# A two-layer decoder trunk on one core: compressed scores, their transposes and the nonlinearity's transposes at other places of a hand-written order, the last squares on DVE, the second weight block as two loads

## The chip, the core and the metric

The kernel runs on one core of a Trainium2 chip. The core has a matrix engine (TensorE, PE, with a separate weight load, PEld), a vector engine (VectorE, DVE), a scalar engine (ScalarE, ACT), a general engine (GpSimd, POOL) and a queue engine (SyncE, SP) that here only issues DMAs. Each engine takes its own instructions in order; engines wait for one another through semaphores. The metric is the device time of one execution in microseconds, as the median over runs.

## What is computed

The input x is 256 tokens by 1024. Layer 0 is stick-breaking attention and a squared-ReLU MLP. After it, shared keys and values are projected for three branches. Layer 1 is native sparse attention (NSA) over these and a second MLP. A last RMSNorm ends the trunk. All data are fp32. The parts that the change touches, cut from the reference:

```
hid   = gelu(einsum('bncgf,cfe->bncge', blk, cmp_w1))       # compressed blocks, hidden layer
cmp   = einsum('bncge,ced->bncgd', hid, cmp_w2)             # k_cmp, v_cmp: 15 blocks of 4 groups
sc    = einsum('bqghd,bngd->bghqn', qg, k_cmp) * scale      # compressed scores
p_cmp = softmax(where(valid_c, sc, NEG))
o_cmp = einsum('bghqn,bngd->bqghd', p_cmp, v_cmp)
...
out   = einsum('bsch,bschd->bshd', gates, [o_cmp, o_sel, o_win])   # sigmoid gates, then @ w_o
h     = h + out @ w_o
h     = h + relu(rms_norm(h, g) @ w1)**2 @ w2
return rms_norm(h, final_norm)                               # h * rsqrt(mean(h*h) + eps) * gain
```

With 256 tokens the selected and the window branch each run over all causal keys, so the kernel computes plain causal softmax scores for both.

## The kernel before

Weights are streamed from HBM by SP in blocks of up to 1 MB (`raw`). Each fp32 block is split into two fp32r tensors: ACT makes the high part (L125, CAST `wh<-raw`), DVE the rest (L126, `wl<-raw,wh`). PE multiplies such products in three passes (L177, L178, L179: high by high, and the two cross products; which of the two operands is the low one differs by the caller). Other products are single fp32 passes (L182), and transposes are matmuls with the identity (L185).

**The start.** `v_load` loads a part of a block of the value weights wv. The block of index 0 holds the rows for k = 0 and k = 1, 1024 columns each; k = 0 is loaded in two halves of 512 columns, k = 1 in one piece. `x_load` loads x by k, ACT and DVE scale and split it (L412, L413), and `pv` is accumulated over k by three matmuls for each of two token tiles and two column halves, twelve for each k. All these loads are issued by SP in the order of the code.

**Layer 1.** The table `NSA` is an order of steps written out by hand, and PE's instructions keep exactly that order (`keep_in_program_order`). The orders of DVE, ACT and POOL come from the scheduler, which places each step's instructions by its own costs. The steps that matter here:

- `('q', g, half)`: half of the query projection of group g, 24 matmuls into `pq`; after the second half ACT copies it to `qu` (L721). `('qr', g)`: rotary tables applied to it (L726 to L730 on DVE, L727 on POOL), giving `qr`.
- `('ge',)`: the nonlinearity of the hidden layer, which ends in `hu` on DVE (L758). `('ch',)`, `cmp_hid`: four PE transposes of hu into `pht` (L765), the copy `hidT` on ACT (L767), and its widened copy `hv` on POOL (L769). `('ck',)`, `cmp_kv`: PE products `pkc` from hidT and `pvc` from hv, then DVE copies to `kcb` (L781) and `vcb` (L788).
- `('cp', hf)`, `cmp_probs`: the compressed scores `psc` of half of the heads on PE, and their softmax: DVE L805, L807, ACT L809 (exponential), DVE L811 to L815, into `ce`. `('ct', hf)`, `cmp_tr`: four PE transposes of ce into `pct` and the ACT copy `pcT` (L824); the second argument names the PSUM pool of pct ("a" or the default "z").
- For each pair p of heads: `('S', p)` scores `z` on PE, each with a mask and minimum on DVE (L857) and an exponential with its sum on ACT (L859); `('M', p)` one over the sums times the gate on DVE (L866, L868, tile `rs`), then four multiplies of the tiles `pe` by rs on POOL (L873); `('T', p)` twelve transposes `ptp` and their copies `pT` (L888 on DVE, L890 on ACT); `('V', p)` the products with the values, into `po`, the last of them with pcT and vcb.
- `('w',)`: one more split of a weight block, `('o', ...)`: the output projection.

**The tail.** The second MLP ends in `finish`, called for each token tile t, each half n of the 1024 columns and each piece q of that half. For the last tile the second half comes as 384 and 128 columns. Each call takes the squares with their sum on ACT (L972) and multiplies by the gain on DVE (L973). After the second half the sum becomes `v` (L978), POOL raises it to the power -0.5 (L983), ACT scales columns 0 to 383 and DVE the other 640 (L985, L986), and ACT and SP issue one output DMA each (L987, L988).

Of the kernel before, what the change touches and what calls it, by code (L numbers as in the profile page):

```python
# [7 lines left out]
F32 = mybir.dt.float32  # L8
F32R = mybir.dt.float32r
BF16 = mybir.dt.bfloat16  # L10
AF = mybir.ActivationFunctionType
OP = mybir.AluOpType
AX = mybir.AxisListType

P = 128
D = 1024
T = 2
# [37 lines left out]
def hybrid_kernel(ctx, tc, x, xcols, eye, gcols, gfin, wqk, wv, wo0, wkv, wq, wg, rot, wo1, w1, w2, cw1, cw2, cpos, gate_b, consts, out):  # L55
    nc = tc.nc

    cp = ctx.enter_context(tc.tile_pool(name="cp", bufs=1))
    wp = ctx.enter_context(tc.tile_pool(name="wp", bufs=3))
    sp = ctx.enter_context(tc.tile_pool(name="sp", bufs=2))  # L60
# [7 lines left out]
    def big(shape, dt, name):  # L68
        return cp.tile(shape, dt, tag="e", name=name, bufs=3)
# [35 lines left out]
    def v_load(j, a, b):  # L105
        nc.sync.dma_start(raws[j][:, a:b], stream[j][0][:, a:b])
# [100 lines left out]
    hres = [cp.tile([P, D], F32, name=f"hres{t}") for t in range(T)]  # L207
# [6 lines left out]
    npow = cst[:, C_PW:C_PW + 1]  # L214
# [165 lines left out]
    def layer0(ap):  # L380
# [5 lines left out]
        v = big([P, T, D], F32, "v0")  # L386
# [15 lines left out]
        def x_load(k, m):  # L402
            nc.sync.dma_start(xin[:, k:k + m, :].rearrange("p k q -> p (k q)"), xcols[:, k * T * P:(k + m) * T * P])
# [17 lines left out]
        v_load(0, 0, 512)  # L421
        v_load(0, 512, D)
        x_load(1, 1)
        v_load(0, D, 2 * D)
        x_load(2, 1)
        v_load(1, 0, D)
        x_load(3, 1)
# [520 lines left out]
    def scoped(f, name, *a, bufs=2):  # L948
        with tc.tile_pool(name=name, bufs=bufs) as ap:
            return f(*a, ap)  # L950

    xn = scoped(layer0, "l0")
    nxt = []

# [8 lines left out]
    gf = big([P, D], F32, "gf")  # L963
# [4 lines left out]
    def finish(i, t, n, q):  # L968
        c = slice(n * 512 + q.start, n * 512 + q.stop)
        j = n + (q.start > 0)  # L970
        ss, sq, y = ssq[t], ys[t][:, 0, :], ys[t][:, 1, :]
        nc.scalar.activation(sq[:, c], hres[t][:, c], AF.Square, accum_out=ss[:, j:j + 1])  # L972
        nc.vector.tensor_mul(y[:, c], hres[t][:, c], gf[:, c])  # L973
        if n == 0:
            nc.vector.tensor_scalar(ss[:, 0:1], ss[:, 0:1], 1.0 / D, EPS, op0=OP.mult, op1=OP.add)
            return
        v = sp.tile([P, 1], F32, name="v", bufs=4)
        nc.vector.scalar_tensor_tensor(v, ss[:, j:j + 1], 1.0 / D, ss[:, 0:1], op0=OP.mult, op1=OP.add)  # L978
        if q.stop < 512:
            nc.vector.tensor_copy(ss[:, 0:1], v)  # L980
            return
        r = sp.tile([P, 1], F32, name="r", bufs=4)
        nc.gpsimd.tensor_tensor(r, v, npow, op=OP.pow)  # L983
        m = 384
        nc.scalar.activation(y[:, 0:m], y[:, 0:m], AF.Copy, scale=r)  # L985
        nc.vector.tensor_scalar(y[:, m:D], y[:, m:D], r, None, op0=OP.mult)  # L986
        nc.scalar.dma_start(out[t * P:(t + 1) * P, 0:m], y[:, 0:m])  # L987
        nc.sync.dma_start(out[t * P:(t + 1) * P, m:D], y[:, m:D])  # L988

    scoped(mlp, "m1", 1, 3, xn, finish)  # L990


# [92 lines left out]
```

## Time and profile before

| | us |
|---|---|
| median of 3 runs | 626.78 (626.08 to 626.88) |
| profiled execution | 626.89 |
| its span on the core | 625.1 |
| PE busy in the span | 613.3 (98%) |
| DVE busy | 416.7 (67%) |
| ACT busy | 344.6 (55%) |
| POOL busy | 54.1 (9%) |
| mean granted PE clock | 0.998 |

A row of a timeline gives the start, the busy time, the engine, the line, the operation, the output and inputs by the program's names, the shapes and the count, and in brackets the idle time before it and what ended it. A row of a view of waits gives who waited for whom, then the total, the times and the longest in microseconds. Line numbers are those of the kernel before; in the changed kernel most stand one higher.

### The profile page before, as it was taken

How to read it: one execution, taken by the hardware profiler on the slowest of the kernel's cores; microseconds unless marked ns; L12 is line 12 of the kernel's file. 1: busy time of each engine (PE TensorE's matmuls, PEld its weight loads, DVE VectorE, ACT ScalarE, POOL GpSimd, SP SyncE). 2: the span in 40 equal slices, each digit the busy share in tenths (PEclk: the TensorE clock that was granted, in tenths of full speed). 3: DMA queues.
4: the chain of work that ended last, by engine and by line, in shares of the span. 5: the costliest groups of instructions: out<-in, count | busy, mean ns of one | idle time of the engine just before them, and what ended most of it. 6: DMA issues, size and time to landing. Idle time of an engine off the chain costs nothing.

```text
span 625.1 us, 9055 instructions
## 1 busy us (share of the span) xinstructions
PE 613.3 (98%) x3555; PEld 516.1 (83%) x3555; DVE 416.7 (67%) x667; ACT 344.6 (55%) x593; POOL 54.1 (9%) x76
## 2 busy tenths in 40 slices
PE   8999999999999999999999998999999999999995
PEld 5899987888888888888888786777888888888885
DVE  5588887766566666656774798854676656666655
ACT  5666666464554444443853686773564455444442
POOL 0100000000000000000321166450000000000000
PEclk9999999999999999999999999999999999999999
DMA  8863333546555455553558511212374555545501
GB/s 299 342 264 136 135 135 135 170 163 207 201 185 204 159 202 193 202 202 135 175 210 329 202 69 69 102 40 96 135 231 174 201 202 190 204 156 201 194 0 68
DMA packets 17755, 108.12 MB, mean 173 GB/s; under 512 B 2352, under 2 KB 3504, under 8 KB 5680
## 3 DMA queue, kind: packets, MB, share of 16 engines
q1 hardware_dynamic: 16416, 105.97, 47.5%
q10 hardware_dynamic: 1296, 1.57, 0.7%
q8 instruction: 28, 0.46, 0.3%
q14 instruction: 15, 0.12, 0.1%
HBM read 106.48 MB, written 1.05 MB: 172 GB/s over the span
## 4 chain that ended last, share of the span: by engine, by line
PE 90%; DVE 4%; ACT 2%; issue 1%; DMA 1%; SPq 0%; POOLq 0%; POOL 0%; DVEq 0%
PE pu L182 29%; PE acc L177 12%; PE acc L178 11%; PE acc L179 11%; PE po L182 3%; PE qk L177 3%; PE qk L179 2%; PE qk L178 2%; PE z L182 2%; PE pk L177 2%; PE pk L178 2%; PE pk L179 2%; PE ptp L185 1%; ACT pe L859 1%; PE ph L182 1%
## 5 line engine op out<-in xcount | busy, mean ns | idle before, releaser
L126 DVE TENSOR_TENSOR wl<-raw,wh 128x1024 fp32r<-128x1024 f32 (+1 forms) x190 | 225.9, 1224 | 124.1 <-ACT wh L125 116.3
L125 ACT CAST wh<-raw 128x1024 fp32r<-128x1024 f32 (+1 forms) x190 | 189.7, 1043 | 104.4 <-PE acc L179 51.1
L182 PE MATMUL pu<-xn,wh 128*128 128x512 f32 x512 | 132.1, 392 | 0.0
L182 PEld LDWEIGHTS pu<-xn,wh 128*128 128x128 f32 x512 | 93.7, 188 | 18.0
L177 PE MATMUL acc<-wh,hh 128*128 128x512 f32 (+1 forms) x256 | 100.2, 391 | 0.0
L178 PE MATMUL acc<-wl,hh 128*128 128x512 f32 (+1 forms) x256 | 99.9, 390 | 0.0
L179 PE MATMUL acc<-wh,hl 128*128 128x512 f32 (+1 forms) x256 | 99.0, 389 | 0.0
L182 PE MATMUL pu<-xn,wl 128*128 128x256 f32 x512 | 76.5, 282 | 0.0
L182 PEld LDWEIGHTS pu<-xn,wl 128*128 128x128 f32 x512 | 72.1, 190 | 5.1
L179 PEld LDWEIGHTS acc<-wh,hl 128*128 128x128 f32 x256 | 48.1, 188 | 10.7 <-DVE hl L355 0.6
L177 PEld LDWEIGHTS acc<-wh,hh 128*128 128x128 f32 x256 | 48.2, 188 | 10.1 <-ACT hh L354 0.9
L178 PEld LDWEIGHTS acc<-wl,hh 128*128 128x128 f32 x256 | 48.2, 188 | 8.7
L354 ACT CAST hh<-ms 128x512 fp32r<-128x512 f32 x32 | 19.8, 620 | 63.0 <-DVE ms L350 63.0
L346 ACT COPY mr<-pu 128x256 f32<-128x256 f32 x64 | 23.6, 368 | 27.7 <-PE pu L182 27.7
L177 PE MATMUL qk<-xa,wh 128*128 128x256 f32 x128 | 37.4, 292 | 0.0
L179 PE MATMUL qk<-xa,wl 128*128 128x256 f32 x128 | 36.3, 284 | 0.0
L178 PE MATMUL qk<-xa,wh 128*128 128x256 f32 x128 | 36.2, 283 | 0.0
L355 DVE TENSOR_TENSOR hl<-ms,hh 128x512 fp32r<-128x512 f32 x32 | 22.1, 691 | 19.2 <-ACT hh L354 19.2
L873 POOL TENSOR_TENSOR pe<-pe,rs 128x512 f32<-128x512 f32 (+1 forms) x32 | 31.4, 1013 | 21.8 <-DVE rs L868 16.4
L859 ACT ACTIVATE pe<-pe,nm 128x256 f32<-128x256 f32 (+1 forms) x64 | 28.3, 443 | 8.4 <-DVE nm L857 7.2
L347 DVE TENSOR_TENSOR mu<-pu,mr 128x256 f32<-128x256 f32 x64 | 26.6, 417 | 7.5 <-ACT mr L346 7.5
L177 PE MATMUL acc<-wh,oT 128*128 128x512 f32 x64 | 26.2, 409 | 0.0
(187 smaller groups left out, 851.0 us busy)
## 6 DMA issues: line engine op xcount, KB each, us to landing
raw<-in_w SPq DMA_DIRECT2D x64, 1024.0 KB, 4.8
raw<-in_wqk SPq DMA_DIRECT2D x8, 1024.0 KB, 4.9
raw<-in_wo SPq DMA_DIRECT2D x8, 1024.0 KB, 4.7
raw<-in_wkv SPq DMA_DIRECT2D x6, 1024.0 KB, 4.9
raw<-in_wq SPq DMA_DIRECT2D x4, 1024.0 KB, 4.9
wc<-in_cw SPq DMA_DIRECT2D x4, 1024.0 KB, 6.7
raw<-in_wv SPq DMA_DIRECT2D x7, 512.0 KB, 8.8
hres<-in_x SPq DMA_DIRECT2D x2, 512.0 KB, 8.9
```

What stands on the lines that cost most here:

```text
L125: nc.scalar.copy(h[:, r], raws[j][:, r])
L126: nc.vector.tensor_sub(lo[:, r], raws[j][:, r], f32(h[:, r]))
L177: pe(nc.tensor.matmul(o, a[0], b[0], start=first, stop=False, skip_group_check=True))
L178: pe(nc.tensor.matmul(o, a[0], b[1], start=False, stop=False, skip_group_check=True))
L179: pe(nc.tensor.matmul(o, a[1], b[0], start=False, stop=last, skip_group_check=True))
L182: pe(nc.tensor.matmul(o, a, b, start=first, stop=last, skip_group_check=True))
L346: nc.scalar.copy(r[:, q], pu[:, 256:512])
L347: nc.vector.tensor_add(u[:, q], pu[:, 0:256], r[:, q])
L354: nc.scalar.copy(hh, sv)
L355: nc.vector.tensor_sub(hl, sv, f32(hh))
L859: nc.scalar.activation(e, e, AF.Exp, scale=-1.0, bias=nm[:, hd, t, b:b + 1], accum_out=rs[:, hd, t, b:b + 1])
L873: nc.gpsimd.tensor_tensor(sv, sv, rs[:, hd, t, :][:, :, None].to_broadcast([P, 2, n]), op=OP.mult)
```

## The change

Three edits. In the table of layer 1, `('ch',)` goes from ahead of `('q', 2, 0)` to behind it, `('cp', 0)` from behind T 1, qr 2 and a weight split to ahead of `('q', 3, 0)`, and `('ct', 0)` from behind `('q', 3, 1)` to ahead of it, with its PSUM tile from the other pool. At the start the load of the second k is issued as two loads of 512 columns. In `finish`, for the second half of the columns one reducing DVE multiply replaces ACT's square, the gain multiply and the tile v; it starts from the sum so far and writes the next one. POOL takes that sum directly. The last scaling is divided at 512 columns instead of 384, and DVE's part now multiplies h by r and the gain in one instruction.

```diff
-    ('cw', 1, 0), ('cw', 1, 1), ('q', 1, 0), ('ge',), ('q', 1, 1), ('S', 0, 'zzaz'), ('M', 0), ('qr', 1), ('ch',),
-    ('q', 2, 0), ('S', 1), ('M', 1), ('ck',), ('q', 2, 1), ('w',), ('T', 0, 'zaa'), ('S', 2, 'azaz'), ('q', 3, 0),
-    ('T', 1), ('qr', 2), ('w',), ('cp', 0), ('M', 2), ('S', 3, 'azaa'), ('q', 3, 1), ('ct', 0, 'a'), ('M', 3), ('V', 0), ('S', 4),
+    ('cw', 1, 0), ('cw', 1, 1), ('q', 1, 0), ('ge',), ('q', 1, 1), ('S', 0, 'zzaz'), ('M', 0), ('qr', 1),
+    ('q', 2, 0), ('ch',), ('S', 1), ('M', 1), ('ck',), ('q', 2, 1), ('w',), ('T', 0, 'zaa'), ('S', 2, 'azaz'), ('cp', 0),
+    ('q', 3, 0), ('T', 1), ('qr', 2), ('w',), ('M', 2), ('S', 3, 'azaa'), ('ct', 0), ('q', 3, 1), ('M', 3), ('V', 0), ('S', 4),
...
-        v_load(0, D, 2 * D)
+        v_load(0, D, D + 512)
+        v_load(0, D + 512, 2 * D)
...
-        nc.scalar.activation(sq[:, c], hres[t][:, c], AF.Square, accum_out=ss[:, j:j + 1])
-        nc.vector.tensor_mul(y[:, c], hres[t][:, c], gf[:, c])
+        hv = hres[t]
         if n == 0:
+            nc.scalar.activation(sq[:, c], hv[:, c], AF.Square, accum_out=ss[:, 0:1])
+            nc.vector.tensor_mul(y[:, c], hv[:, c], gf[:, c])
             nc.vector.tensor_scalar(ss[:, 0:1], ss[:, 0:1], 1.0 / D, EPS, op0=OP.mult, op1=OP.add)
             return
-        v = sp.tile([P, 1], F32, name="v", bufs=4)
-        nc.vector.scalar_tensor_tensor(v, ss[:, j:j + 1], 1.0 / D, ss[:, 0:1], op0=OP.mult, op1=OP.add)
+        nc.vector.tensor_tensor_reduce(sq[:, c], hv[:, c], hv[:, c], 1.0 / D, ss[:, j - 1:j], OP.mult, OP.add, ss[:, j:j + 1])
         if q.stop < 512:
-            nc.vector.tensor_copy(ss[:, 0:1], v)
             return
         r = sp.tile([P, 1], F32, name="r", bufs=4)
-        nc.gpsimd.tensor_tensor(r, v, npow, op=OP.pow)
-        m = 384
+        nc.gpsimd.tensor_tensor(r, ss[:, j:j + 1], npow, op=OP.pow)
+        m = 512
         nc.scalar.activation(y[:, 0:m], y[:, 0:m], AF.Copy, scale=r)
-        nc.vector.tensor_scalar(y[:, m:D], y[:, m:D], r, None, op0=OP.mult)
+        nc.vector.scalar_tensor_tensor(y[:, m:D], hv[:, m:D], r, gf[:, m:D], op0=OP.mult, op1=OP.mult)
```

What the table makes of the engines' queues is seen at three places. First POOL, between the rotary product of group 1 (L727, in the changed kernel L728) and the multiplies of M1 (the last row). The tiles pe_3233 and pe_3234 before, pe_3234 and pe_3235 after, are those of M0. Before:

```order
L727 TENSOR_TENSOR qr_2659<-qu_2658,cs_2646 128x512 x2
L769 COPY hv_3269<-hidT_3267 128x480
L873 TENSOR_TENSOR pe_3233<-pe_3233,rs_3232 128x512
L873 TENSOR_TENSOR pe_3234<-pe_3234,rs_3232 128x512
L873 TENSOR_TENSOR pe_3233<-pe_3233,rs_3232 128x256
L873 TENSOR_TENSOR pe_3234<-pe_3234,rs_3232 128x256
L873 TENSOR_TENSOR pe_3310<-pe_3310,rs_3309 128x512
```

Of the change:

```order
L728 TENSOR_TENSOR qr_2660<-qu_2659,cs_2647 128x512 x2
L874 TENSOR_TENSOR pe_3234<-pe_3234,rs_3233 128x512
L874 TENSOR_TENSOR pe_3235<-pe_3235,rs_3233 128x512
L874 TENSOR_TENSOR pe_3234<-pe_3234,rs_3233 128x256
L874 TENSOR_TENSOR pe_3235<-pe_3235,rs_3233 128x256
L770 COPY hv_3299<-hidT_3297 128x480
L874 TENSOR_TENSOR pe_3311<-pe_3311,rs_3310 128x512
```

The copy hv moved from ahead of the four multiplies of M0 to behind them. Second PE, from the last matmul of q(2,0) to the first of q(2,1) in the changed kernel:

```order
L179 MATMUL pq<-xq,wl 128x256
L766 MATMUL pht<-ident,hu 128x60 x4
L182 MATMUL z_3301<-kT,qr 128x512
L182 MATMUL z_3302<-kT,qr 128x512
L182 MATMUL z_3303<-kT,qr 128x256
L182 MATMUL z_3304<-kT,qr 128x256
L182 MATMUL pkc<-hidT,w2d 128x60 x2
L182 MATMUL pvc<-cw2s,hv 60x64 x8
L177 MATMUL pq<-xq,wh 128x256
```

Before, the transposes pht stood ahead of q(2,0), so that its 24 matmuls came between pht and these four scores of S1; now only the four scores stand between pht and the products with hidT and hv. Third DVE, at the softmax of the first compressed scores. Before:

```order
L805 TENSOR_REDUCE cmx<-psc 128x16
L868 TENSOR_TENSOR rs<-rs,gates 128x8
L807 TENSOR_TENSOR ce<-psc,cmx 128x240
L857 ISA pe,nm<-z_3513,nmask 128x256
L857 ISA nm 128x1
L857 ISA pe,nm<-z_3513,nmask 128x256
L857 ISA nm 128x1
L811 TENSOR_REDUCE csm<-ce 128x16
```

Of the change, as far as the multiply that ends it:

```order
L806 TENSOR_REDUCE cmx<-psc 128x16
L727 STREAM_SHUFFLE qx<-qu 128x512
L808 TENSOR_TENSOR ce<-psc,cmx 128x240
L730 TENSOR_TENSOR qx<-qx,cs 128x512
L126 TENSOR_TENSOR wl<-raw,wh 128x1024
L812 TENSOR_REDUCE csm<-ce 128x16
L889 COPY pT<-ptp 128x512
L813 RECIPROCAL csm<-csm 128x16
L731 TENSOR_TENSOR qr<-qr,qx 128x512
L814 TENSOR_TENSOR csm<-csm,gates 128x16
L867 RECIPROCAL rs<-rs 128x8
L816 TENSOR_TENSOR ce<-ce,csm 128x240
```

Before, the steps of the softmax stood among the masked scores (L857) of S3; now the rotary steps of group 2, a weight split and a copy of pT stand between them, and S3's follow it.

## The prediction

> **What bounds the kernel now.** I read the page first, then TensorE's (PE's) waits where layer 1's order is edited, then the timelines of the engines it waits for, then the two ends.
>
> ```profile
> span 625.1 us, 9055 instructions
> PE 613.3 (98%) x3555; PEld 516.1 (83%) x3555; DVE 416.7 (67%) x667; ACT 344.6 (55%) x593; POOL 54.1 (9%) x76
> PE 90%; DVE 4%; ACT 2%; issue 1%; DMA 1%; SPq 0%; POOLq 0%; POOL 0%; DVEq 0%
> ```
>
> PE is busy 98% of the span and carries 90% of the chain that ended last. The change leaves its work as it is, so a change of time can only come from PE's few gaps, from new gaps, and from the two ends. In the edited stretch of layer 1 (356 to 392 us) the waits of PE and the busy times (PE, weight load, DVE, ACT, POOL; clock 1.00) are:
>
> ```profile
> PE pht L765 <- DVE hu L758: 1.3, 1, 1.3
> PE po L182 <- ACT pcT L824: 1.3, 1, 1.3
> PE pct L185 <- DVE ce L815: 0.3, 1, 0.3
> 356.00:392.00 36.00, 33.13 (x263) 26.04 (x261) 32.61 (x122) 29.13 (x96) 21.34 (x20) 1.00 0.23 86
> ```
>
> DVE, at 32.6 of 36 us, is almost as full as PE, and POOL, 9% over the span, is 59% busy here. An average over the whole kernel hides that. PE's timeline of the stretch:
>
> ```profile
> 358.96 0.46 PE L765 MATMUL pht<-ident,hu 60*128 60x60 f32 x4 [1.29 <-DVE hu L758]
> 359.35 0.38 PE L177 MATMUL pq<-xq,wh 128*128 128x256 f32 x1
> ...
> 362.41 1.56 PE L182 MATMUL z<-kT,qr 64*128 64x512 f32 x8
> 363.90 0.66 PE L182 MATMUL pkc<-hidT,w2d 128*128 128x60 f32 x4
> 364.49 1.10 PE L182 MATMUL pvc<-cw2s,hv 128*60 128x64 f32 x16
> ...
> 374.36 1.47 PE L185 MATMUL ptp<-ident,pe 128*128 128x128 f32 x12
> ...
> 377.38 0.28 PE L182 MATMUL psc<-cmb,cbf 128*128 128x120 bf16 x2
> 377.58 2.18 PE L182 MATMUL z<-kT,qr 64*128 64x512 f32 x8
> ...
> 383.14 0.60 PE L185 MATMUL pct<-ident,ce 128*60 128x128 f32 x4 [0.31 <-DVE ce L815]
> ...
> 386.45 0.65 PE L182 MATMUL po<-pcT,vcb 128*64 128x256 f32 x4 [1.26 <-ACT pcT L824]
> ```
>
> PE loses four pieces: 1.29 ahead of the transposes of the hidden layer (pht), 2.18 - 1.56 = 0.62 inside the scores of pair 3, 0.31 ahead of pct, and 1.26 ahead of the products with pcT. Together 3.48 us.
>
> **The change part by part.** *Layer 1's order.* The half projection q(2,0) lasts 362.41 - 359.35 = 3.06 us and now stands ahead of the transposes. It covers the 1.29 us in which hu is late. What is late next is what the transposes start: hidT on ACT, then hv on POOL, which pkc and pvc need. Before, q(2,0) and S1 (3.06 + 1.5 us of PE) stood between; now S1 alone does.
>
> ```profile
> 362.22 0.34 ACT L767 COPY hidT<-pht 128x240 f32<-128x240 f32 x1
> 362.46 1.05 ACT L125 CAST wh<-raw 128x1024 fp32r<-128x1024 f32 x1
> ```
> ```profile
> 361.00 1.20 DVE L126 TENSOR_TENSOR wl<-raw,wh 128x1024 fp32r<-128x1024 f32 x1
> ...
> 363.03 0.57 DVE L868 TENSOR_TENSOR rs<-rs,gates 128x8 f32<-128x8 f32 x1
> ...
> 363.92 1.34 DVE L730 TENSOR_TENSOR qr<-qr,qx 128x512 f32<-128x512 f32 x1
> ...
> 369.29 2.34 DVE L126 TENSOR_TENSOR wl<-raw,wh 128x1024 fp32r<-128x1024 f32 x2
> ```
> ```profile
> 362.62 0.94 POOL L769 COPY hv<-hidT 128x480 f32<-128x480 f32 x1 [2.44 <-ACT hidT L767]
> 363.68 3.63 POOL L873 TENSOR_TENSOR pe<-pe,rs 128x512 f32<-128x512 f32 x4
> 369.51 5.17 POOL L873 TENSOR_TENSOR pe<-pe,rs 128x512 f32<-128x512 f32 x4 [2.20 <-DVE rs L868]
> ```
> ```profile
> 379.55 3.18 POOL L873 TENSOR_TENSOR pe<-pe,rs 128x512 f32<-128x512 f32 x4 [3.62 <-DVE rs L868]
> ```
>
> On ACT the cast wh now stands ahead of hidT, so hidT is ready near 362.3 + 1.05 + 0.34 = 363.6 instead of 362.56. That alone would cost PE little, as pkc started at 363.90. POOL is the place that counts. Its rows above show that hv, which stood ahead of the four multiplies of M0, now stands behind them, and POOL takes its instructions in order. M0 needs rs (L868, begun at 363.03; its row lasts to 363.60, with hv running beside it). M0 then starts between 363.1 and 363.68, and I take 363.3. Its four multiplies last 3.18 us where DVE leaves them alone, 3.63 beside one L730, and 5.17 beside two L126 of 2.34 us. DVE now does one L126 and a L729 and L730 in that time. So I add 5.17 - 3.18 = 1.99 for two L126, that is 1.0 for one, and 0.2 for part of the 0.45 of L730. hv, 0.94, ends at 363.3 + 3.18 + 1.2 + 0.94 = 368.6. The lower bound is 363.1 + 3.18 + 0.94 = 367.2, the upper 363.68 + 5.17 + 0.94 = 369.8. pvc began at 364.49 before; it is **4.1 us** later (2.7 to 5.3). All of PE queues behind it: q(2,1), the transposes T0, S2.
>
> [...]
>
> While PE stands, DVE, ACT and POOL go on. The three later gaps, 0.62 + 0.31 + 1.26 = 2.19 us, are then recovered, and two edits help there: the scores psc move ahead of q(3,0), T1 and S3, and q(3,1), about 3 us, now covers the copy of pcT. Against that, the softmax chain of ce now shares DVE with L726, L729, an L126, L888 and L730 between its steps. It took 383.14 - 377.66 = 5.5 us from the end of psc to pct before. What covers it now is q(3,0), T1 and S3, 3.06 + 1.3 (T1's transposes, the row at 374.36) + 1.56 = 5.9 us, and one L126 is already 1.2 us more chain. I take 0.6 us of new waits there and at the later transposes (0 to 1.2: at the low end they fall into slack, at the high end the L126 lies in the chain whole). Pool z for pct instead of pool a costs no instruction.
>
> Layer 1's stretch: 4.1 - 2.19 + 0.6 = **+2.5 us** (0.5 to 4.3).
>
> *Second weight block in two.*
>
> ```profile
> 2.58 0.43 SPq L106 DMA_DIRECT2D raw<-in_wv  x1
> ```
> ```profile
> 4.32 0.62 ACT L125 CAST wh<-raw 128x512 fp32r<-128x512 f32 x1 [2.30 <-DMA raw<-in_wv]
> ...
> 8.82 1.14 ACT L125 CAST wh<-raw 128x512 fp32r<-128x512 f32 x2 [0.77 <-DMA raw<-in_wv]
> ```
> ```profile
> 9.49 1.02 PE L177 MATMUL pv<-wh,xa 128*128 128x512 f32 x3 [1.23 <-ACT wh L125]
> 10.36 0.40 PE L178 MATMUL pv<-wl,xa 128*128 128x512 f32 x1
> ...
> 12.44 0.84 PE L177 MATMUL pv<-wh,xa 128*128 128x512 f32 x3
> ```
>
> ACT idled 0.77 us for the block, so its cast could start at 8.05 at the earliest. With the first half landed midway the cast ends near 8.8, and the rest wl 0.7 later, about 9.5. PE's first matmul moves up, but the second needs wl: 9.53 plus 11 matmuls at (12.44 - 10.36) / 9 = 0.23 us ends at 12.05 instead of 12.44. That is **-0.4 us** (-0.5 to 0, the latter if the first half lands no earlier). The extra issue of 0.43 us on SP delays the second half and the loads queued behind it, x_load(2,1) first; the second half has six matmuls, 1.4 us, of cover, and without that the 0.43 would eat the gain.
>
> *Tail.*
>
> ```profile
> 618.35 0.28 PE L179 MATMUL accq<-wh,hl 128*128 128x128 f32 x1
> ```
> ```profile
> 619.00 0.15 DVE L980 COPY ssq<-v 128x1 f32<-128x1 f32 x1
> 619.07 0.34 DVE L268 SCALAR_TENSOR_TENSOR hres<-accq,r,hres 128x128 f32<-128x128 f32 x1
> 619.44 0.29 DVE L973 TENSOR_TENSOR ys<-hres,gf 128x128 f32<-128x128 f32 x1
> ```
> ```profile
> 620.12 0.55 POOL L983 TENSOR_TENSOR r<-v,cst 128x1 f32<-128x1 f32 x1 [5.22 <-DVE v L978]
> ```
> ```profile
> 620.70 0.62 ACT L985 ACTIVATE ys<-ys,r 128x384 f32<-128x384 f32 x1 [0.85 <-POOL r L983]
> 621.34 0.36 ACTq L987 DMA_DIRECT2D out<-ys  x1
> ```
>
> PE ends at 618.63, but the last residual (L268) starts at 619.07 behind v and L980, both gone. I put it at 618.7. One reducing multiply of 128 columns replaces ACT's square, its read, and v: priced by L973's 0.29 for the same shape, plus a read of 0.1, so POOL's power starts near 619.45 instead of 620.12. The last scaling grows from 384 to 512 columns, at most 0.62 x 512/384 = 0.83. Net -0.67 + 0.15: **-0.5 us** (-0.65 to -0.2).
>
> Sum against the profiled execution, 625.1 in the span and 626.89 in all: +2.5 - 0.4 - 0.5 = +1.6, so 628.5. It stands 0.1 above the median of the runs, 626.78, hence **628.4**.
>
> **The rivals.** *No change:* POOL is free of DVE, hv comes at its lower bound, and no new wait shows. Then layer 1 costs 2.7 - 2.19 = 0.5, less 0.9 at the ends: 626.4. With half a microsecond of contention or of waits left, about 627.2. For it: the four multiplies do run in 3.18 us where DVE is elsewhere. Against: DVE is 91% busy here, with two L126 due near. *Faster:* POOL does not hold pvc at all, because hv gets through before M0; then all of the 3.48 us go and the ends add 0.9: 622.5. It decides as soon as hv ends by 364.5, as before. For it speaks that hidT is ready at 363.6, with POOL idle at that moment if rs is late. Against it: an engine's queue does not overtake. *A cascade:* M0 and hv block L729 and L730 on DVE in turn (1.34 us in the row above), which delays S1's exponentials, M1 and ce; pvc at its upper bound and 1.2 us of waits give 5.3 - 2.19 + 1.2 = +4.3, less 0.9 or less: 630.2 to 630.9. For it: DVE has 3.4 us free in 36. Against: PE stands for 4 us meanwhile and gives DVE time to catch up.
>
> **How the numbers follow.** Forecast (a long stall at pvc, the later gaps recovered) 0.45, no change 0.30, cascade 0.17, faster 0.08. A measurement of this kernel tells a difference of about 0.2%, or 1.25 us, so "same" is 625.5 to 628.0. Slower holds the cascade and most of the forecast, 0.17 + 0.38 = 0.55; same holds the rest of the forecast and the no-change case, 0.37; faster 0.08. The forecast alone runs from 627.5 to 629.5; to hold eight in ten I go down to the no-change case, 626.6, and up to just under the cascade, 630.2.
>
> **What would show it.** Right: PE's wait ahead of pht is gone, and a wait of about 4 us stands at pvc, released by POOL's hv near 368.6; the 1.26 us at po<-pcT is gone; the first long wait of the start is 0.6 us shorter; the last DMA is issued about 2.2 us after PE's last matmul instead of 2.7. Wrong: pvc starts by 366, or hv stands ahead of M0 on POOL in the trace (then faster), or new waits over 1.2 us at pct, S3 or the ptp transposes (then the cascade). If the start or the tail moves by more than half a microsecond the other way, those terms were mis-sized.

## The result, and the profile after

| | before | changed |
|---|---|---|
| median of 6 runs each, us | 626.83 (626.08 to 627.0) | 631.13 (629.87 to 632.04) |
| ratio | 1 | 1.007 (95% interval 1.0057 to 1.0083) |
| profiled execution, us | 626.89 | 629.87 |
| span, us | 625.1 | 628.0 |
| mean granted clock of PE | 0.998 | 0.991 |

The change made the kernel 4.3 us slower. The forecast of 628.4 had the direction, and the range ended at 630.2, below the result. First PE's waits of the changed kernel in the stretch of layer 1 (350 to 400 us):

```profile
PE pvc L182 <- POOL hv L770: 4.4, 1, 4.4
PE pkc L182 <- ACT hidT L768: 1.1, 1, 1.1
PE ptp L185 <- DVE nm L858: 0.7, 1, 0.7
```

The waits at pht, at pct and at the products with pcT are gone, and the wait at pvc is there. In PE's timeline:

```profile
355.16 1.56 PE L182 MATMUL z<-kT,qr 64*128 64x512 f32 x8
...
362.60 0.66 PE L182 MATMUL pkc<-hidT,w2d 128*128 128x60 f32 x4 [1.08 <-ACT hidT L768]
367.63 1.96 PE L182 MATMUL pvc<-cw2s,hv 128*60 128x64 f32 x16 [4.38 <-POOL hv L770]
...
369.52 0.58 PE L177 MATMUL pq<-xq,wh 128*128 128x256 f32 x1
...
373.33 1.47 PE L185 MATMUL ptp<-ident,pe 128*128 128x128 f32 x12
```

Layer 1's first scores start at 355.16 instead of 356.11, so all of this stretch is to be read 0.95 us earlier. The rows of before for this are:

```profile
356.11 1.56 PE L182 MATMUL z<-kT,qr 64*128 64x512 f32 x8
...
368.49 1.47 PE L185 MATMUL ptp<-ident,pe 128*128 128x128 f32 x12
```

Against the first scores pvc starts 12.47 us later instead of 8.38 (364.49 - 356.11): 4.1 us later, just as worked out. But the same matmuls of pvc (eight, which the trace shows as sixteen records) now last 1.96 us instead of 1.10, and from pvc to the transposes ptp it is 5.70 us where it was 4.00 (364.49 to 368.49). The same work on PE takes 1.70 us longer, with no wait in it. The windows tell why (the columns are those of the prediction's window: busy times of PE, PEld, DVE, ACT, POOL, then the granted clock, the share of DMA and GB/s):

```profile
362.00:367.00 5.00, 0.66 (x4) 0.52 (x4) 4.91 (x19) 2.17 (x9) 4.63 (x5) 0.76 0.52 162
367.00:368.00 1.00, 0.37 (x4) 0.37 (x5) 0.56 (x5) 1.00 (x5) 0.57 (x2) 0.50 0.57 238
...
370.00:371.00 1.00, 1.00 (x7) 1.00 (x7) 1.00 (x5) 0.00 (x0) 0.00 (x0) 0.50 0.00 0
371.00:372.00 1.00, 1.00 (x8) 1.00 (x8) 0.18 (x2) 0.00 (x0) 0.68 (x1) 0.79 0.00 0
372.00:373.00 1.00, 1.00 (x11) 1.00 (x10) 0.00 (x0) 0.00 (x0) 1.00 (x2) 1.00 0.04 8
```

While PE stood, its granted clock fell to 0.50, and it came back only at about 371.4, after 3.8 us of work at 0.50. POOL's queue is what held hv:

```profile
362.37 4.66 POOL L874 TENSOR_TENSOR pe<-pe,rs 128x512 f32<-128x512 f32 x4 [3.14 <-ACT wh L125]
366.98 0.59 POOL L770 COPY hv<-hidT 128x480 f32<-128x480 f32 x1
```

M0 takes 4.66 us (I had 3.18 + 1.2) and hv 0.59 (I had 0.94). The start and the tail:

```profile
11.46 0.84 PE L177 MATMUL pv<-wh,xa 128*128 128x512 f32 x3
...
621.58 0.28 PE L179 MATMUL accq<-wh,hl 128*128 128x128 f32 x1
```
```profile
624.09 0.38 ACTq L987 DMA_DIRECT2D out<-ys  x1
```

k = 2 starts at 11.46 instead of 12.44 in this execution. The last output DMA is issued 624.09 - 621.86 = 2.23 us after PE's last matmul, instead of 621.34 - 618.63 = 2.71.

### The profile page after: what moved, and what is told of

Same layout as the page of the kernel before. It is cut to its first block, busy times and chain, and to the rows that moved or that the text cites. A ratio compares the mean times of both kernels' runs of the same rounds, so it can differ in the third digit from the quotient of the medians.

```text
span 628.0 us, 9044 instructions
## 1 busy us (share of the span) xinstructions
PE 614.5 (98%) x3555; PEld 518.2 (83%) x3555; DVE 414.4 (66%) x666; ACT 343.3 (55%) x587; POOL 53.9 (9%) x76
## 4 chain that ended last, share of the span: by engine, by line
PE 93%; ACT 2%; DVE 2%; issue 1%; POOL 1%; POOLq 0%; DVEq 0%; ACTq 0%
PE pu L182 28%; PE acc L177 11%; PE acc L178 11%; PE acc L179 11%; PE po L182 3%; PE qk L177 3%; PE qk L179 2%; PE qk L178 2%; PE z L182 2%; PE pk L177 2%; PE pk L178 2%; PE pk L179 2%; PE ptp L185 2%; PE pv L177 1%; PE pv L178 1%; PE pv L179 1%
```

## The experiments

The theory after the result: the stall at pvc costs what was forecast, and the half clock behind it is the rest. The rival: contention between DVE and POOL and a late softmax, the cascade of the prediction, make up the excess. For the comparison of profiles the time from the first scores of layer 1 to the start of the last matmul serves best (S0 to end below), since it leaves out start and tail; it is worked out from the two rows in each trace (before: 618.35 - 356.11 = 262.24).

| kernel | median, us | before beside it | ratio (95%) | S0 to end, us |
|---|---|---|---|---|
| changed | 631.13 | 626.83 | 1.007 (1.0057 to 1.0083) | 266.42 |
| e2_keep_warm | 628.72 | 626.58 | 1.004 (1.0025 to 1.0055) | 264.79 |
| e2b_half_warm | 629.04 | 626.46 | 1.0038 (1.0025 to 1.0052) | 264.81 |
| e2c_four_warm | 631.15 | 626.53 | 1.0074 (1.0059 to 1.0089) | 266.80 |
| e1_hv_first | 624.81 | 626.58 | 0.9976 (0.9967 to 0.9985) | 260.85 |
| e3_ch_back | 625.16 | 626.58 | 0.9981 (0.9971 to 0.999) | 261.26 |
| e4_ch_only | 630.75 | 626.58 | 1.0074 (1.0059 to 1.0089) | 266.68 |
| e5_start_only | 626.37 | 626.46 | 0.9998 (0.9989 to 1.0007) | 262.22 |
| e6_tail_only | 626.22 | 626.46 | 0.9995 (0.9986 to 1.0004) | 262.14 |
| e11_q_ahead_ck | 624.48 | 626.46 | 0.997 (0.9958 to 0.9981) | 262.00 |
| e12_t2_banks | 624.83 | 626.53 | 0.9971 (0.996 to 0.9983) | 260.92 |

**Keeping PE at work during the stall.**

```diff
             pvc = bank("pvc")
+            for _ in range(18):
+                mm(pvc, zero[:, 0:P], zero, True, True)
```

> The change with 18 matmuls of zeros (bf16, 128x512) between pkc and pvc, written into the bank of pvc before its own products; TensorE has work while it would wait for hv. Theory of the clock: the wait of 4.4 us at pvc lets the granted clock fall to 0.50, and that adds about 1.7 us behind it (pvc 1.96 instead of 1.10, q(2,1) 3.81 instead of 2.97). With the dummies the granted clock stays at 1.00, pvc takes 1.1 and the time falls by 1.7 us or more, to 628.4 to 629.4, though pvc starts no earlier than 367.6. Rival, contention between DVE and POOL and a late softmax chain: nothing on TensorE matters, the time stays at 630.5 to 631.5.

Measured 628.72, 2.4 us less than the change. PE's timeline and two windows of this kernel:

```profile
363.89 0.66 PE L182 MATMUL pkc<-hidT,w2d 128*128 128x60 f32 x4 [1.08 <-ACT hidT L768]
364.38 4.05 PE L182 MATMUL pvc<-zero 128*128 128x512 bf16 x18
368.92 1.10 PE L182 MATMUL pvc<-cw2s,hv 128*60 128x64 f32 x16 [0.48 <-POOL hv L770]
...
372.94 1.47 PE L185 MATMUL ptp<-ident,pe 128*128 128x128 f32 x12
```
```profile
362.00:368.00 6.00, 4.92 (x27) 2.42 (x24) 5.76 (x17) 3.17 (x11) 4.33 (x4) 1.00 0.33 106
368.00:372.00 4.00, 3.52 (x36) 3.01 (x34) 2.48 (x14) 2.28 (x12) 2.00 (x4) 1.00 0.27 109
```

Against the first scores (356.45) pvc starts as late as in the change, 12.47 us, and still POOL releases it. The clock stays at 1.00, pvc takes 1.10 and from pvc to ptp it is 4.02 us again. The stall alone is worth 264.79 - 262.24 = 2.55 us, the half clock 266.42 - 264.79 = 1.63 us in these two profiles, and 4.30 - 2.14, about 2.2 us, by the medians, each against the before beside it. The rival of contention falls: up to hv, DVE and POOL do the same in both kernels (M0 takes 4.66 us in both).

**Fewer matmuls of zeros.** The same with 9 and with 4 of them, which makes PE's pause longer.

> The change with 9 matmuls of zeros between pkc and pvc instead of 18: TensorE still stands 1.1 us at pkc and about 2.4 us at pvc. If the clock falls only after a stretch with next to no work that is longer than these, it stays at 1.00 and the time is that of 18 matmuls, 628.7. If any pause over 2 us lowers it, pvc takes 1.96 again and the time is 630 to 631.

> The change with 4 matmuls of zeros between pkc and pvc: TensorE stands 1.1 us at pkc and about 3.5 at pvc, between the 2.4 that left the clock at 1.00 and the 4.4 that halved it. If the pause needed lies above 3.5, the clock stays and the time is 628.7 to 629.0; if it lies between 2.4 and 3.5, pvc takes up to 1.96 and the time is 630 to 631.

With 9, PE stood 2.43 us ahead of pvc, the clock stayed at 1.00 and the time was 629.04, as with 18. With 4 it stood 3.51 us, pvc took 1.96 again, and the time was 631.15, as with none:

```profile
368.70 1.10 PE L182 MATMUL pvc<-cw2s,hv 128*60 128x64 f32 x16 [2.43 <-POOL hv L770]
```
```profile
368.49 1.96 PE L182 MATMUL pvc<-cw2s,hv 128*60 128x64 f32 x16 [3.51 <-POOL hv L770]
```

Windows in the pause, with 9 and then with 4:

```profile
366.00:369.00 3.00, 0.57 (x7) 0.31 (x6) 2.64 (x19) 2.56 (x11) 2.64 (x4) 1.00 0.75 306
```
```profile
366.00:366.50 0.50, 0.00 (x0) 0.00 (x0) 0.50 (x5) 0.26 (x1) 0.50 (x1) 0.68 0.57 180
```

A pause of 2.43 us left the clock at 1.00, and with one of 3.51 us it fell. The length of the pause by itself can't have decided it: with 4 matmuls PE went idle at 368.49 - 3.51 = 364.98, and 0.68 over half a microsecond puts the fall near 366.2, only 1.2 us later. What differs is what PE had done just before, 4 matmuls of zeros (1.03 us) or 9 (2.11 us). Whether that decided it these runs do not show: in three executions of the changed kernel itself the fall came 1.4 to 2.4 us after PE went idle (below).

**Is it the same every time?** The changed kernel was profiled twice more.

> The changed kernel once more, for a second profile. Its executions spread over 2.2 us where those of before spread over 0.9. If the half clock behind the pause is what varies, the stretch at 0.50 to 0.55 behind pvc is longer or shorter than the 3.9 us of the first profile, up to 6, and the time from the first scores of layer 1 to the last matmul changes by half of the difference. If it does not vary, that time is 266.4 us again and the spread comes from elsewhere.

> A third profile of the changed kernel, with the same two readings as for the second.

Times 631.28 and 630.48, S0 to end 267.00 and 266.67. Windows of the first of the two:

```profile
362.00:367.00 5.00, 1.03 (x8) 0.52 (x4) 4.76 (x13) 2.17 (x7) 3.76 (x3) 0.95 0.29 80
367.00:368.00 1.00, 0.00 (x0) 0.00 (x0) 1.00 (x9) 1.00 (x5) 1.00 (x3) 0.50 0.98 418
...
372.00:373.00 1.00, 1.00 (x7) 1.00 (x6) 0.04 (x1) 0.00 (x0) 0.81 (x1) 0.50 0.00 0
373.00:374.00 1.00, 1.00 (x9) 1.00 (x9) 0.00 (x0) 0.00 (x0) 1.00 (x2) 0.82 0.02 8
```

PE's timeline of the same execution, then of the second:

```profile
368.49 1.96 PE L182 MATMUL pvc<-cw2s,hv 128*60 128x64 f32 x16 [4.37 <-POOL hv L770]
...
374.66 1.47 PE L185 MATMUL ptp<-ident,pe 128*128 128x128 f32 x12
```
```profile
368.05 1.96 PE L182 MATMUL pvc<-cw2s,hv 128*60 128x64 f32 x16 [4.38 <-POOL hv L770]
...
373.96 1.47 PE L185 MATMUL ptp<-ident,pe 128*128 128x128 f32 x12
```

Windows of the second:

```profile
362.00:367.00 5.00, 0.66 (x4) 0.52 (x4) 4.91 (x16) 2.17 (x7) 4.20 (x4) 0.85 0.35 115
...
372.00:373.00 1.00, 1.00 (x9) 1.00 (x8) 0.00 (x0) 0.00 (x0) 1.00 (x2) 0.82 0.03 8
```

A mean clock of 0.95 over 5 us is 0.5 us at half, so the fall was near 366.5; 0.82 over 1 us puts the return near 373.4. That is 6.8 to 6.9 us at half clock. The first profile gives 364.6 to 371.4 in the same way (0.76 over 5 us, 0.79 over 1), and the last one 365.5 to 372.4 (0.85 and 0.82). The length is 6.8 us each time, but it starts 1.4, 2.4 and 1.8 us after PE went idle behind pkc (pvc's start less the wait in its row), so 3.8, 4.9 and 4.3 us of it fall on work (the "up to 6" of the expectation was the author's estimate). From pvc to ptp it is 5.70, 6.17 and 5.91 us instead of 4.00, longer by 1.7, 2.2 and 1.9: a little less than half of those stretches. This is a part of the spread of 2.2 us among the runs of the change. The half clock also lasts 6.8 us in the traces of e2c_four_warm and e4_ch_only, where PE stands 3.5 and 4.4 us.

These stretches are the whole excess over a kernel with the clock at 1.00. If what the stretch from pvc to ptp lasts above 4.00 us is taken off S0 to end, the three profiles of the change give 264.72, 264.83 and 264.76, and e2c_four_warm (2.01 us above) gives 264.79. The two kernels whose clock stayed at 1.00 stand at 264.79 and 264.81. Nothing of the excess is left for contention or a late softmax.

What sets the start and the length of these stretches is not shown. PE had not been idle for long ahead of them: pkc, 0.66 us of work, ended 1.4, 2.4 and 1.8 us before the three falls.

**hv ahead of M0.**

```diff
-    ... ('S', 0, 'zzaz'), ('M', 0), ('qr', 1),
-    ('q', 2, 0), ('ch',), ('S', 1), ...
+    ... ('S', 0, 'zzaz'), ('qr', 1),
+    ('q', 2, 0), ('ch',), ('M', 0), ('S', 1), ...
```

> The change with M0 behind the transposes in the table, so that POOL takes hv ahead of M0's multiplies and TensorE's order is as in the change. Theory that hv behind M0 is the whole loss: the wait at pvc shrinks from 4.4 to under 0.6 us, the 1.1 us for hidT at pkc stays, the clock stays at 1.00, and the time is 624.2 (623.5 to 625.5), below the kernel before. Rival, that M0 put off by hv makes the transposes T0 wait and DVE and POOL block each other: 626 to 628, with a new wait of over 1 us at ptp.

Measured 624.81, 1.8 us below before and 6.3 below the change, with PE's order unchanged. POOL and PE:

```profile
363.19 0.60 POOL L770 COPY hv<-hidT 128x480 f32<-128x480 f32 x1 [3.36 <-ACT hidT L768]
363.75 3.19 POOL L874 TENSOR_TENSOR pe<-pe,rs 128x512 f32<-128x512 f32 x4
```
```profile
362.00:368.00 6.00, 4.91 (x48) 4.61 (x47) 5.62 (x29) 4.81 (x19) 3.74 (x5) 1.00 0.01 3
```
```profile
363.85 1.10 PE L182 MATMUL pvc<-cw2s,hv 128*60 128x64 f32 x16
```

The wait at pvc is nil and the clock 1.00. Against the first scores (355.73) M0 starts 8.02 us later, 0.8 us more than in the change, and beside other work of DVE (5.62 of the 6.00 us above) it took 3.19 instead of 4.66 us; putting it off cost nothing. So hv's place behind M0 is what costs: with it set right the rest of the table is a gain, 262.24 - 260.85 = 1.39 us. The edit also moves DVE's steps: in the window from 362 to 368 the row above has 29 of them, the row of e2_keep_warm 17. The 1.1 us at pkc stay, as expected, and 0.5 us at pct and 0.7 at ptp are there too.

**The transposes back, the rest of the table kept; and the transposes alone.**

```diff
-    ... ('M', 0), ('qr', 1),
-    ('q', 2, 0), ('ch',), ('S', 1), ...
+    ... ('M', 0), ('qr', 1), ('ch',),
+    ('q', 2, 0), ('S', 1), ...
```

(e3_ch_back, applied to the changed kernel; e4_ch_only is the reverse, applied to the kernel before.)

> The change with the hidden layer's transposes back ahead of q(2,0); the compressed scores, pct, the start and the tail as in the change. If moving psc and pct removes the later gaps by itself (the wait for ce, the wait for pcT, S3's), the 1.3 us at pht stays and layer 1 gains 1.0 to 1.6: 624.2 (623.8 to 624.8). If those gaps went in the change only because TensorE stood still for hv, layer 1 gains nothing, and only the start (0.95) and the tail (0.5) are left: 625.4.

> The kernel before with the hidden layer's transposes alone moved behind q(2,0). The loss alone: 4.1 us of later pvc and 1.7 us of half clock. If TensorE's standing still is what lets the other engines catch up, 2 us of later gaps go: 630.6. If the moves of psc and pct are what removes them, they stay: 632.6.

e3_ch_back came to 625.16, above the 623.8 to 624.8 of the first reading and nearer to the 625.4 of the second, so the time alone does not choose. The trace does: S0 to end is 261.26, 0.98 us less than before, and the three profiles with layer 1 as before (before, e5, e6) agree within 0.10 us. Moving psc and pct thus removes later gaps by itself, about the low end of the 1.0 to 1.6; a wait for ce of 0.5 us and one at ptp of 0.7 are new. What the time lacks is at the start and the tail, counted in the second reading at over 1 us; alone they show 0.1 and 0.3 us (the next runs).

e4_ch_only came to 630.75, the 630.6 of the first reading: with PE standing still the gaps inside S3 and at pct go without any other edit. By the traces it is 262.24 + 4.09 (pvc later) + 1.61 (half clock) - 266.68 = 1.26 of the 2 us, and this wait stays:

```profile
PE po L182 <- ACT pcT L824: 1.1, 1, 1.1
```

The two gains are thus not added up: psc and pct are worth 0.98 us without the stall and about 0.3 us with it (266.68 - 1.61 = 265.07 in e4_ch_only, against the 264.72 to 264.83 above).

**The start and the tail alone.**

> The kernel before with the second weight block alone loaded in two. The prediction gave the start 0.4 us; the profiled execution of the change reached the first scores of layer 1 0.95 us earlier, but e4_ch_only, which has the start of before, reached them 0.38 us earlier too. If the 0.38 is a difference between executions, the gain is 0.4 to 0.6 and the time 0.9993 of before (626.1 beside 626.6). If the whole 0.95 is the edit's, the ratio is 0.9985.

> The kernel before with the new tail alone. The prediction gave it 0.5 us: the last output DMA is issued 2.2 us after TensorE's last matmul instead of 2.7, ratio 0.9992. If the end of the execution hangs on the landing of the output DMAs and not on their issue, the ratio is 1.000.

Neither can be told from no change: 0.9998 and 0.9995, with intervals of about 0.0009 to each side. That rules out the 0.9985 for the start, but not its 0.9993. The tail's profile shows what was expected (the last DMA is issued 2.23 us after the last matmul), and 0.0005 of 626.5 is 0.3 us, so the 0.5 is neither confirmed nor ruled out. For the start the traces vary. Eleven profiled executions with the load in two reached the first scores at 355.16 to 356.45 (mean 355.68), and three with one load at 355.60 to 356.11 (mean 355.81: before, e4, e6). In three of the eleven the next block (k = 2) was late instead, by 0.6 to 1.0 us, as in e2_keep_warm:

```profile
12.32 0.96 PE L177 MATMUL pv<-wh,xa 128*128 128x512 f32 x3 [0.96 <-ACT wh L125]
```

**Two attempts at more.** Both start from e1_hv_first. One puts q(2,1) ahead of pkc and pvc, the other gives T2 its tiles from pools a, a, z.

```diff
-    ('M', 1), ('ck',), ('q', 2, 1), ('w',), ...          # e11_q_ahead_ck
+    ('M', 1), ('q', 2, 1), ('ck',), ('w',), ...
...
-    ('T', 2, 'aza')                                      # e12_t2_banks
+    ('T', 2, 'aaz')
```

> e1_hv_first with q(2,1) ahead of pkc and pvc, so that 3 us of TensorE cover the copies hidT and hv. If the 1.1 us at pkc is then the only thing that changes, 623.7 (1.1 less than the 624.8 of e1_hv_first). Rival: the widened values vcb and the cast behind come late on DVE, the first softmax of the compressed scores or the transposes wait instead, and the time is 624.5 or more.

> e1_hv_first with the PSUM pools of T2's three tiles in the order a, a, z instead of a, z, a. It has a wait of 0.7 us at its second tile, for DVE to be done with a tile of pool z. If the tile of pool z is free by the time of the third, 0.4 us later, the wait falls to 0.3 or nothing and the time by 0.3 to 0.7, to 624.2; if pool a is not free for the second, the wait moves there and nothing is gained.

624.48 and 624.83: neither can be told from e1_hv_first. In e11_q_ahead_ck the wait at pkc is gone and two others take its place. The transposes wait, as in the rival, but for POOL's multiplies, and the scores for ACT's copy, not for the values on DVE:

```profile
PE ptp L185 <- POOL pe L874: 0.8, 1, 0.8
PE z L182 <- ACT pT L891: 0.7, 1, 0.7
```

Its profile, of the slowest of its six executions (625.49), holds another half clock:

```profile
370.82 1.97 PE L182 MATMUL psc<-kcb,qu 128*128 128x30 f32 x16
```
```profile
373.00:374.00 1.00, 1.00 (x7) 1.00 (x6) 1.00 (x11) 1.00 (x5) 0.00 (x0) 0.52 0.00 0
...
376.00:377.00 1.00, 1.00 (x8) 1.00 (x8) 1.00 (x2) 0.30 (x2) 0.00 (x0) 0.77 0.00 0
```

The clock stood at 0.50 from about 373.0 to 376.5, and the half projection q(3,0) took 4.46 us instead of 2.96 in e1_hv_first. These 1.5 us are in the 262.00 of the table. No long pause led to it: the longest wait near it is the 0.8 us above, and in a stretch of the same length before the fall (3.4 us) PE's rows are busy for 2.85 us, most of it the matmuls of 30 columns (psc). What made the clock fall here stays open, and so does whether the other five executions had it.

In e12_t2_banks the wait at ptp fell from 0.7 to 0.3 us, and S0 to end stayed at 260.9: by the output projection behind T3 the two kernels are level again (37.33 us from the first scores in e1_hv_first, 37.35 here), with no wait in the rows that explains it.

## Why the prediction was wrong

- **The stall at pvc: right.** "pvc began at 364.49 before; it is 4.1 us later": 4.1 us, released by hv behind M0 on POOL, as the queues showed. Within it M0 was longer and hv shorter than taken (4.66 and 0.59 against 4.38 and 0.94), which cancelled by luck. One reading in it was wrong, at no cost here: "That alone would cost PE little" compared hidT with pkc's old start, but S1 now ends earlier, and PE waits 1.1 us at pkc; e1_hv_first keeps that wait.
- **The recovered gaps and the new waits: right.** "4.1 - 2.19 + 0.6 = +2.5 us" is what the kernel with PE kept at work shows, 2.55. The new wait came at the transposes ptp (0.7) and not at pct.
- **What failed** is that this sum was taken for the whole of "Layer 1's stretch". It priced a stall of PE by its length alone, and named only its good side ("PE stands for 4 us meanwhile and gives DVE time to catch up"). It lacked a term for what a pause does to PE's own clock. The keep-warm kernel shows that term at 1.63 us in the profiles and about 2.2 by the medians, and the three profiles of the change show 1.7 to 2.2 us. With these the forecast of 628.4 becomes 630.1 to 630.6. The rest to 631.13 is of the size of what the two ends were credited with and did not show (0.9 us against 0.1 and 0.3). The rows read before had the clock at 1.00 in this stretch and no pause over 1.3 us; a clock read from a kernel without such a pause could not carry to one with it.
- **The start: mis-sized.** "-0.4 us (-0.5 to 0)" measured as 0.1 us with an interval of 0.6 to each side. k = 1 does end earlier: k = 2 starts at 11.40 in e5_start_only instead of 12.44. But the load for k = 2 is issued at 4.00 in the change instead of 3.53, and in three executions PE waited 0.6 to 1.0 us for it. The text named the loads behind the extra issue and put no price on them.
- **The tail: right in the profile, unproved in the time.** Expected -0.5; 0.48 us less from the last matmul to the last issue, and 0.9995 in the runs.
- **The cascade** had the number nearest to the result, 630.2 to 630.9, with the wrong mechanism: no extra waits on DVE or at ce made it. **No change** (0.30) and **faster** (0.08) did not come: M0 took 4.66 us, not 3.18, and hv did not get past M0 (hidT was done at 362.55, M0's four multiplies ran from 362.37 to 367.03, and hv began at 366.98). The 3.18 of before was not taken with DVE at rest either: it was busy for 3.12 of these 3.18 us (379.55 to 382.73), with the masks (L857) and the softmax of ce.

## What to carry to other kernels

When a wait on the matrix engine moves or grows, price it twice: its length, and the work that may then run at half clock, at a little less than half of that stretch (here 1.7 to 2.2 us behind a pause of 4.4, 2.0 behind 3.5, nothing behind 2.4). These runs give no limit for a safe pause, so read the granted clock in the new kernel's own trace. Look at the in-order queue of an engine that is nearly idle by the page: POOL, at 9% of the span, decided this change because one copy of 0.6 us went behind four multiplies. And a hand-written order that only constrains one engine also sets the others' priorities, so moving one more step (M0 behind the transposes) turned a loss of 4.3 us into a gain of 1.8.

## What the runs showed of the hardware that was not expected

The granted clock of PE fell to 0.50 soon after PE had still done 0.66 us of work (pkc), and in e2c_four_warm even 1.03 us more of zeros. It fell 1.2 to 2.4 us after PE went idle, while a pause of 2.43 us in e2b_half_warm left it at 1.00, and in e11_q_ahead_ck it fell with no wait above 0.8 us near it. The half clock lasted 6.8 us in each of the three profiles of the change, of which at least 3.8 us were dense work, and 3.4 us in e11_q_ahead_ck. Counted from the moment PE went idle, the fall moved by about 1 us between executions of one kernel. Matmuls of zeros were enough to hold the clock at 1.00 through the stall, 18 of them (4.05 us) and also 9 (2.11 us).
